# Expert stages of an eight-stage transformer stack: weights in 8 KB runs, the gather of the next pair inside this pair's products, the overflow blocks ahead of the last pair, the residual in the router

## The chip, the cores and the metric

The kernel runs on one core of one Trainium2 chip. Its time is the device time of one execution in microseconds (us). Before the change three runs gave a median of 2939.56 us (2938.95 to 2942.76).

## The reference

The model is a stack on 256 tokens of 1024 features: two layers of (feed-forward, token mix, feed-forward), then (state space mixer, mixture of experts) and (dilated attention, mixture of experts). The change lies in the two mixture stages alone. Each computes, with 32 experts of hidden size 512:

```python
g_w, g_idx = lax.top_k(jax.nn.softmax(g_logits, axis=-1), 1)        # one of 4 groups
e_logits = e_logits[jnp.arange(t), g_idx[:, 0]]                     # its 8 experts
e_w, e_idx = lax.top_k(jax.nn.softmax(e_logits, axis=-1), MOE_TOP_K)  # two of them
e_w = e_w / jnp.sum(e_w, -1, keepdims=True)
gates = (g_w * e_w).reshape(-1)
...
def expert_block(args):
    xb, e = args
    h = jax.nn.silu(xb @ w_gate[e]) * (xb @ w_up[e])
    return h @ w_down[e]
...
ffn = _hierarchical_moe(x, ...)
x = _layer_norm_2(DEEPNORM_ALPHA * x + ffn, ln_g[i, 1], ln_b[i, 1])
```

All weights are float32: three matrices of 2 MB for each expert, 201 MB for a stage.

## The kernel before, in words

Activations lie with features on partitions, `X["T"]` as 8 chunks of 128 features by 256 tokens, and as high and low parts `X["h"]`, `X["l"]`. A stage (`moe`) goes like this.

**Router.** Sixteen products per stage (L1302, L1303) make the logits while the chunks of x come out of the layer norm before; `lf` takes them to SBUF, `lgt` and `xtp` are transposes that put the logits and x itself with tokens on partitions (`xt`). From the choice of experts DVE works out `rk`, the place of each token in its expert's list, and `gt`, its weight. `warm` issues idle products on TensorE.

**Pairs.** The 32 experts go in 16 pairs (indices 0 to 15), each expert with 64 places. For a pair, `run` issues in program order:
- the gather `xgp` (L1455): x of the tokens in the two lists, by one-hot products with `ot`, in two halves of four 128x128 chunks. One logical product of 32-bit numbers is two records in the trace. Each half goes to `xg` by a copy on DVE (L1460). Before the first pair is done, it goes in pieces of one chunk, alternately on DVE and ScalarE;
- the transposes of the weighted lists, `ogp` (L1463), copied to `og` by ScalarE (L1465);
- the gate and up products (L1478) into the sums `gps` and `ups`: two halves of the features, in each half gates, then ups, four chunks each. The first expert uses columns 0 to 63 of the array and the second columns 64 to 127: `[128*64]` in the trace, the two alternating in the program and running at the same time in the trace;
- tanh on ScalarE (L188), two multiplications on DVE (L1493, L1494) into `t`, four transposes `htp` (L1497), a copy to `hT` on DVE (L1499);
- the down products `yp` (L1510), 16 logical products in two output halves, again two experts side by side, copied to `y` by ScalarE (L1519);
- `eacc` (L1535): eight products that add the weighted rows into the sums of the stage, which stay in PSUM.

PSUM holds four banks of sums, one each for `gps` and `ups`, and two buffers of one bank (pool `em`, tag `m`) that `xgp`, `ogp`, `htp` and `yp` share in turn. `xg` and `y` share one buffer (tag `xy`).

**Residual.** x times ALPHA is put into the sums by 16 products with `alphas` (L1437), issued inside pair 0, some around its `htp` and the rest behind its `yp`.

**Weights.** For a pair 12 tiles of 1 MB are loaded by SyncE (L1564 gate and up, L1571 down) into a ring of 21 buffers, whose order is `ORDER` (L23). The view `(c p) m -> p c m` puts rows p, p+128, ... on partition p, so one run in memory is one row: 2 KB of gate or up, 4 KB of down. A load waits until the products that read its buffer before are done.

**Overflow.** `more()` (an If with a loop over blocks, L1594) handles experts with more than 64 tokens. It is written after pair 10 (`MOREQ`). Its body takes six buffers of the ring when the program is built, executed or not; in this run no body is executed in either stage.

**Last pair.** In pair 15 the mean for the next layer norm (`meanp`) is worked out too, and the products into the sums are in high and low parts.

The order in which each engine gets its instructions is set when the program is built: a scheduler takes instructions by its own estimates of when each can start, so instructions that are written one after the other can be interleaved.

Of the kernel before, what the change touches and what calls it, by code (L numbers as in the profile page):

```python
# [10 lines left out]
F32 = mybir.dt.float32  # L11
# [20 lines left out]
W1 = 0  # L32
# [15 lines left out]
def tile_stack(ctx: ExitStack, tc: tile.TileContext, a: dict, out: bass.AP):  # L48
# [43 lines left out]
    def project_group(tiles, ws):  # L92
        """up to four chunks at once, (wh, wl, width) each; features outermost, so that it can start on the first."""
# [96 lines left out]
    def table(name):  # L190
        """the functions' tables, loaded behind the last tanh."""
# [4 lines left out]
    def warm(out, n, after):  # L196
        """the array's clock falls in a pause: idle products, into a sum not in use, keep it up."""
# [5 lines left out]
    def last_chunks(accs, ks, first):  # L203
        """the products of the last chunks, (wh, wl, mh, ml) each, into one output chunk."""
# [113 lines left out]
    def ffn(l, w1, w2, g, b, setup=None):  # L318
        with pool(name="accps", bufs=1, space=PSUM) as aps, pool(name="gups", bufs=2, space=PSUM) as gps, \
# [26 lines left out]
            def gate_up(js):  # L346
                """the hidden chunks js; features outermost, so that it can start on the first of them."""
# [42 lines left out]
    def log1p_exp_neg_abs(pool, x, shape, tag):  # L390
        """log(1 + exp(-|x|)) by the series of atanh."""
# [34 lines left out]
    def bias_tile(pool, h, queue=None, bufs=3):  # L426
        """T[q, k] = rel[bucket(128 + q - k), h], with the mask of the head's kind."""
# [48 lines left out]
    def token_mix(l):  # L476
        w_in, w_gate, w_out = a["w_in"][l], a["w_gate"][l], a["w_out"][l]
        with ExitStack() as st:
# [25 lines left out]
            def split_pair(t0, t1, c0):  # L504
                """stationary columns: 64 of t0, 64 of t1."""
# [19 lines left out]
            def k_pad(ps, kz, i):  # L525
                """a projected pair of keys into two tiles, each with zeros in the other's rows."""
# [10 lines left out]
            def v_tok(ps, v, i):  # L537
                """keys on partitions: v[:, tile, i, :]."""
# [7 lines left out]
            # compressed keys and values  # L546
# [28 lines left out]
            def compress(i, ts):  # L575
                """four products side by side, then their sum."""
# [26 lines left out]
            # compressed keys  # L603
# [23 lines left out]
            # compressed values  # L627
# [15 lines left out]
            # gates of the three branches and the forget gate  # L643
# [15 lines left out]
            # the running sums of the forget gates  # L659
# [9 lines left out]
            # attention over the compressed blocks, all heads at once  # L669
# [29 lines left out]
            def attend(q, kz, bias, sink=None, gate=None):  # L699
                """probabilities of one head, keys on partitions: [k0 x (q0 q1) | k1 x q1]."""  # L700
# [27 lines left out]
            def pv(po, jobs):  # L728
                """jobs[g]: list of (v of tile 0, v of tile 1 or None, probabilities)."""
# [55 lines left out]
            # NSA  # L785
# [17 lines left out]
            # sliding window with sinks  # L803
# [20 lines left out]
            # forgetting attention  # L824
# [79 lines left out]
    def rsqrt_tile(pool, v, eps, n=S):  # L904
        """(v + eps) ** -0.5, refined by a step of Newton's."""
# [9 lines left out]
    def ssd(g, b):  # L915
        w_in, w_out = a["ssd_w_in_2"][0], a["ssd_w_out_2"][0]
        with ExitStack() as st:
# [13 lines left out]
            def conv(ps, c, dst):  # L931
                """causal convolution of four taps, then twice its silu."""
# [9 lines left out]
            # the keys and queries of the states, B and C  # L942
# [6 lines left out]
            # steps, decays and their running sums  # L949
# [47 lines left out]
            def mix(j, xs, csb, y):  # L997
                """the states' sums for two heads."""
# [115 lines left out]
            # sin, with its sign by row, and cos, one where nothing turns  # L1114
# [136 lines left out]
    NE, CAP, HID, NOV = 32, 64, 512, 7  # L1251
    AHEAD = 7
    MOREQ = 10
# [18 lines left out]
    def router_parts(rp, l):  # L1272
        """the router's weights, high and low parts side by side."""
# [5 lines left out]
    def moe(l, g_, b_, rs, write=False):  # L1279
        w_g, w_u, w_d = a["moe_w_gate_2"][l], a["moe_w_up_2"][l], a["moe_w_down_2"][l]  # L1280
        with ExitStack() as st:
# [17 lines left out]
            # router  # L1299
            ps = mp.tile([72, S], F32, tag="m", name="lgp")  # L1300
            for c in range(KC):
# [7 lines left out]
            warm(accs[0][:, 0, :], W1, x)  # L1309
            # the groups' logits, filled up to eight, then the experts'  # L1310
# [7 lines left out]
            def top(x, name):  # L1318
                """the eight highest logits in order, and where they stand."""
# [8 lines left out]
            # the experts of the other groups far below  # L1328
# [8 lines left out]
            # which experts  # L1337
# [22 lines left out]
            warm(accs[0][:, 0, :], W2, x)  # L1360
# [6 lines left out]
            def weights():  # L1367
                """of the experts chosen."""
# [27 lines left out]
            def beyond():  # L1396
                """blocks of 64 places beyond an expert's first"""
# [33 lines left out]
            def residual():  # L1431
                """x * ALPHA, before the first pair."""
                if "r" not in done:
                    done["r"] = True
                    for c in range(KC):
                        for i in range(2):
                            x = nc.tensor.matmul(out=accs[c // 2][:, c % 2, i * 128:(i + 1) * 128], lhsT=xt[:, i, c * 128:(c + 1) * 128],  # L1437
                                                 rhs=alphas, start=(c % 2 == 0 and i == 0), stop=False, skip_group_check=True)
                            tc.add_manual_dep(x.ins, done["up"].ins.name, order, reason="gates first")

# [5 lines left out]
            def run(os, ogs, loads, n, last):  # L1446
                """n experts of 64 places: os[i], the places of the tokens of half i; ogs[i] with their weights."""
                P = n * CAP
                wg, wu, wd = loads
                xg = wk.tile([128, KC, 128], F32, tag="xy", name="xg", bufs=1)  # L1450
                for q in range(2):
                    ps = mp.tile([128, 4, 128], F32, tag="m", name="xgp")
                    for c in range(4):
# [3 lines left out]
                        if "r" not in done:  # L1457
                            first_copy(c % 2)(out=xg[:, q * 4 + c, 0:P], in_=ps[:, c, 0:P])
                    if "r" in done:
                        nc.vector.tensor_copy(out=xg[:, q * 4:q * 4 + 4, 0:P], in_=ps[:, :, 0:P])  # L1460
# [267 lines left out]
```

## Time and profile before

| | |
|---|---|
| median of 3 runs | 2939.56 us |
| span of the profiled execution | 2939.3 us |
| granted TensorE clock, mean | 0.988 |
| TensorE busy | 2802.7 us, 95% |
| VectorE, ScalarE, GpSimd busy | 1421.7, 1050.9, 196.5 us |
| bytes moved | 697 MB, 237 GB/s over the span |

The page gives for the profiled execution its span, from the first to the last instruction, and no time of its own beside it: 0.3 us under the median of the runs, so that terms of the trace can be added to either. The expert stages are the stretches from about 1684 to 2200 us and from about 2404 to 2920 us. In a row of the timeline the first two numbers are the start in us and the length of the (merged) records, and the bracket at its end is the idle time of the engine before it and what ended it. Matmuls are pipelined, and their ends are modelled, so the distance between starts is what a product costs.

### The profile page before, as it was taken

Reading aid. Unit: us, or ns where it says so; the run is one execution under the profiler, and the core shown is the slowest. Engines: PE = TensorE matmul, PEld = TensorE weight load, DVE = VectorE, ACT = ScalarE, POOL = GpSimd, SP = SyncE. Lnnn points to the kernel's source line nnn. Section 1 sums busy time; section 2 is a strip of 40 time slices with the busy share of each in tenths; the row PEclk is TensorE's granted clock in tenths of the full one; section 3 lists DMA queues with packets and bytes.
Section 4 is the critical chain, followed back from the end, with each engine's and each line's share of the span. In section 5 each row is a group of like instructions: output and inputs, shape, how many; then the busy total and the mean of one; then the engine's idle time right before and its main releaser. Section 6 shows DMA issues by size and latency. Waiting matters only on the chain. (4 is left out here: it accounts for less than half of the span.)

```text
span 2939.3 us, 46679 instructions
## 1 busy us (share of the span) xinstructions
PE 2802.7 (95%) x19161; PEld 2199.8 (75%) x19161; DVE 1421.7 (48%) x3075; ACT 1050.9 (36%) x1949; POOL 196.5 (7%) x263
## 2 busy tenths in 40 slices
PE   8899999999999999999999999999998989999998
PEld 8798899999999889999989854454448974444454
DVE  5466665755655765665688731111127762111113
ACT  4344555544544454544477510000015530000002
POOL 2102000200201100020100100000001010000000
PEclk9899999999999999999999999999999999999999
DMA  8666454455454745445455699998985479999896
GB/s 223 193 201 158 126 159 138 156 184 185 149 194 137 186 130 167 153 139 193 131 194 180 229 364 393 395 393 323 393 305 169 137 256 356 394 393 393 300 394 230
DMA packets 426793, 697.44 MB, mean 237 GB/s; under 512 B 19460, under 2 KB 238384, under 8 KB 426576
## 3 DMA queue, kind: packets, MB, share of 16 engines
q1 hardware_dynamic: 414976, 677.62, 66.3%
q10 hardware_dynamic: 9296, 11.66, 1.3%
q0 software_dynamic: 2304, 5.15, 1.2%
q8 instruction: 152, 2.49, 0.4%
q14 instruction: 65, 0.53, 0.1%
HBM read 693.25 MB, written 4.27 MB: 237 GB/s over the span
## 5 line engine op out<-in xcount | busy, mean ns | idle before, releaser
L84 DVE TENSOR_TENSOR whl<-w,whl 128x1024 fp32r<-128x1024 f32 x487 | 591.5, 1220 | 349.2 <-ACT whl L83 344.2
L83 ACT ACTIVATE whl<-w 128x1024 fp32r<-128x1024 f32 x487 | 507.3, 1050 | 355.9 <-PE gu L113 105.8
L111 PE MATMUL pp<-xh,whl 128*128 128x256 f32 x1432 | 418.1, 292 | 9.0 <-ACT xh L307 4.0
L112 PE MATMUL pp<-xl,whl 128*128 128x256 f32 x1432 | 418.7, 292 | 1.0 <-DVE xl L308 1.0
L113 PE MATMUL pp<-xh,whl 128*128 128x256 f32 x1432 | 412.8, 288 | 0.4 <-DVE whl L510 0.4
L111 PE MATMUL gu<-xh,whl 128*128 128x256 f32 x1408 | 401.6, 286 | 9.9 <-DVE h L361 7.2
L113 PE MATMUL gu<-xh,whl 128*128 128x256 f32 x1408 | 401.4, 285 | 0.5 <-DVE whl L84 0.5
L112 PE MATMUL gu<-xl,whl 128*128 128x256 f32 x1408 | 401.6, 285 | 0.0
L111 PEld LDWEIGHTS pp<-xh,whl 128*128 128x128 f32 x1432 | 274.6, 192 | 17.4 <-ACT xh L307 5.7
L112 PEld LDWEIGHTS pp<-xl,whl 128*128 128x128 f32 x1432 | 275.0, 192 | 10.0 <-issue 6.9
L111 PEld LDWEIGHTS gu<-xh,whl 128*128 128x128 f32 x1408 | 272.8, 194 | 12.2 <-ACT whl L83 9.4
L113 PEld LDWEIGHTS pp<-xh,whl 128*128 128x128 f32 x1432 | 274.6, 192 | 4.3 <-issue 2.4
L112 PEld LDWEIGHTS gu<-xl,whl 128*128 128x128 f32 x1408 | 273.0, 194 | 0.8 <-DVE xl L308 0.7
L113 PEld LDWEIGHTS gu<-xh,whl 128*128 128x128 f32 x1408 | 272.9, 194 | 0.8 <-DVE whl L84 0.8
L1460 DVE COPY xg<-xgp 128x512 f32<-128x512 f32 x60 | 41.5, 692 | 358.5 <-PE xgp L1455 358.5
L111 PE MATMUL acc<-hhi,whl 128*128 128x256 f32 x704 | 201.7, 287 | 2.4 <-DVE rT L231 2.2
L112 PE MATMUL acc<-hlo,whl 128*128 128x256 f32 x704 | 200.1, 284 | 0.0
L113 PE MATMUL acc<-hhi,whl 128*128 128x256 f32 x704 | 199.1, 284 | 0.0
L1493 DVE SCALAR_TENSOR_TENSOR t<-t,gps 128x512 f32<-128x512 f32 x32 | 22.0, 688 | 324.4 <-ACT t L188 324.4
L1519 ACT ACTIVATE y<-yp 128x512 f32<-128x512 f32 x60 | 35.8, 597 | 347.7 <-PE yp L1510 347.7
L111 PEld LDWEIGHTS acc<-hhi,whl 128*128 128x128 f32 x704 | 135.8, 193 | 5.4 <-DVE rT L231 4.0
L112 PEld LDWEIGHTS acc<-hlo,whl 128*128 128x128 f32 x704 | 135.8, 193 | 0.2
(571 smaller groups left out, 5063.0 us busy)
## 6 DMA issues: line engine op xcount, KB each, us to landing
w<-in_ffn_w_dram SPq DMA_DIRECT2D x130, 1024.0 KB, 5.3
wa<-in_moe_w_up_dram SPq DMA_DIRECT2D x48, 1024.0 KB, 14.2
whl<-in_moe_w_down_dram SPq DMA_DIRECT2D x47, 1024.0 KB, 14.1
wa<-in_moe_w_gate_dram SPq DMA_DIRECT2D x43, 1024.0 KB, 14.2
whl<-in_moe_w_gate_dram SPq DMA_DIRECT2D x39, 1024.0 KB, 14.1
wa<-in_moe_w_down_dram SPq DMA_DIRECT2D x37, 1024.0 KB, 13.4
whl<-in_moe_w_up_dram SPq DMA_DIRECT2D x36, 1024.0 KB, 14.2
w<-in_moe_w_down_dram SPq DMA_DIRECT2D x32, 1024.0 KB, 14.4
```

The costliest lines, as they stand in the source:

```text
L83: after_norm(nc.scalar.activation(out=hi, in_=w, func=AF.Copy), nc.vector.tensor_tensor(out=lo, in0=w, in1=hi.bitcast(F32), op=ALU.subtract))
L84: nc.vector.tensor_tensor(out=lo, in0=w, in1=hi.bitcast(F32), op=ALU.subtract))
L111: nc.tensor.matmul(out=o, lhsT=wh, rhs=xh, start=first, stop=False, skip_group_check=skip)
L112: nc.tensor.matmul(out=o, lhsT=wh, rhs=xl, start=False, stop=False, skip_group_check=skip)
L113: return nc.tensor.matmul(out=o, lhsT=wl, rhs=xh, start=False, stop=last, skip_group_check=skip)
L1460: nc.vector.tensor_copy(out=xg[:, q * 4:q * 4 + 4, 0:P], in_=ps[:, :, 0:P])
L1493: nc.vector.scalar_tensor_tensor(out=t[0:P], in0=t[0:P], scalar=1.0, in1=gps[0:P], op0=ALU.add, op1=ALU.mult)
L1519: nc.scalar.activation(out=y[0:P, hs], in_=yp[0:P], func=AF.Copy)
```

## The change

Four things are changed in the expert stages; elsewhere the diff only drops comments.

1. The view of the weights is `(p c) m -> p c m`: rows 4p to 4p+3 (gate, up; 2p and 2p+1 for down) lie on partition p, one run of 8 KB. Products then sum over features in another order, so the eviction of `xtp` to `xt` permutes (ScalarE reads PSUM with a stride of four), and `htp` transposes every second column of `t`.
2. The gather of pair q+1 is issued inside `run` of pair q: the first half behind the tanh, copied to `xg` by ScalarE, the second behind the copy to `hT`, copied by DVE. `ogp` comes behind `hT` (before the gates in the last pair alone). `y` moves to the buffers of `t` and `hT`, `xg` has one of its own.
3. `more()` stands ahead of pair 15, behind the last loads, and its gathered x takes a seventh buffer of the ring.
4. The residual is eight products of `alphas` with `X["T"]` (128x256) among the products of the router; the idle products ahead of them (`W1 = 0`) are gone, those behind (`W2`) write into a sum of their own.

```diff
             for c in range(KC):
                 nc.tensor.matmul(out=ps, lhsT=rs[:, c, :], rhs=X["h"][:, c, :], ...)
                 nc.tensor.matmul(out=ps[0:36], lhsT=rs[:, c, 0:36], rhs=X["l"][:, c, :], ...)
+                if c >= 2:
+                    residual(c - 2)
...
-                    nc.scalar.activation(out=xt[:, i, q * 512:(q + 1) * 512], in_=pt.rearrange("p c t -> p (c t)"), func=AF.Copy)
+                    nc.scalar.activation(out=xt[:, i, q * 512:(q + 1) * 512].rearrange("p (k f) -> p k f", k=4),
+                                         in_=pt.rearrange("p c t -> p (c t)").rearrange("p (f k) -> p k f", k=4), func=AF.Copy)
...
+            def gather(os, P, xg):
+                def half(q):
+                    ps = mp.tile([128, 4, 128], F32, tag="m", name="xgp")
+                    first = "r" not in done
+                    for c in range(4):
+                        for i in range(2):
+                            nc.tensor.matmul(out=ps[:, c, 0:P], lhsT=xt[:, i, (q * 4 + c) * 128:(q * 4 + c + 1) * 128], rhs=os[i], ...)
+                        if first:
+                            first_copy(c % 2)(out=xg[:, q * 4 + c, 0:P], in_=ps[:, c, 0:P])
+                    if not first:
+                        first_copy(1 - q)(out=xg[:, q * 4:q * 4 + 4, 0:P], in_=ps[:, :, 0:P])
+                return [lambda q=q: half(q) for q in range(2)]
...
                 tanh(out=t[0:P], in_=gps[0:P], scale=0.5)
+                if then:
+                    then.pop(0)()
...
-                    nc.tensor.transpose(ht[:, c, 0:P], t[0:P, c * 128:(c + 1) * 128], ident[0:P, 0:P])
+                    nc.tensor.transpose(ht[:, c, 0:P], t[0:P, c // 2 * 256 + c % 2:(c // 2 + 1) * 256:2], ident[0:P, 0:P])
                 hT = wk.tile([128, 4, 128], F32, tag="hT", name="hT", bufs=1)
                 nc.vector.tensor_copy(out=hT[:, :, 0:P], in_=ht[:, :, 0:P])
+                if then:
+                    then.pop(0)()
+                if not last:
+                    ogp = mp.tile([128, S], F32, tag="m", name="ogp")
...
-                residual()
+                done["r"] = True
                 for c in range(KC):
                     combine(c)
...
-    ... w[k][h * 512:(h + 1) * 512, :].rearrange("(c p) m -> p c m", p=128))
+    ... w[k][h * 512:(h + 1) * 512, :].rearrange("(p c) m -> p c m", p=128))
...
-                if q == MOREQ:
-                    more()
+                if q == NP - 1:
+                    more()
```

The order on TensorE shows what the scheduler makes of it. First a pair from the middle of a stage, from the end of one pair's sums (`eacc`) into the gates of the next; W names the buffer that a weight lies in (`w`, `wa`, `whl`), and a DMAHW wait is for its load. Before:

```order
L1535 MATMUL eacc_19046<-og,y 128x256 x2
L1455 MATMUL xgp<-ot,xtok 128x128 [waits PE_49]
L1455 MATMUL xgp<-ot,xtok 128x128 x7
L1455 MATMUL xgp<-ot,xtok 128x128 [waits PE_49]
L1455 MATMUL xgp<-ot,xtok 128x128 x7
L1463 MATMUL ogp<-ident,ogt 128x128 [waits DVE_49]
L1463 MATMUL ogp<-ident,ogt 128x128
L1478 MATMUL gps<-w,xg 64x512 [waits DMAHW1_49]
L1478 MATMUL gps<-w,xg 64x512 [waits DMAHW2_49]
L1478 MATMUL gps<-w,xg 64x512 x6
```

After, the gates of a pair with an index from 6 to 14 in the first expert stage (7 to 14 in the second):

```order
L1549 MATMUL eacc_19046<-og,y 128x256 x2
L1482 MATMUL gps<-whl,xg 64x512 [waits DMAHW5_49]
L1451 MATMUL xgp<-ot,xtok 128x128 [waits PE_49]
L1482 MATMUL gps<-whl,xg 64x512 [waits DMAHW6_49]
L1482 MATMUL gps<-whl,xg 64x512 x6
L1451 MATMUL xgp<-ot,xtok 128x128 x2
L1482 MATMUL ups<-whl,xg 64x512 [waits DMAHW7_49]
L1451 MATMUL xgp<-ot,xtok 128x128 x5
L1482 MATMUL ups<-whl,xg 64x512 [waits DMAHW0_49]
L1482 MATMUL ups<-whl,xg 64x512 x6
L1482 MATMUL gps<-whl,xg 64x512 [waits DMAHW1_49]
```

The first half of the next gather stands in pieces of one, two and five products inside the gate and up products, behind the first expert's first gate and first up product, ahead of the second expert's.

Second, the place behind the up products of a pair, before:

```order
L1497 MATMUL htp<-ident,t 128x128 [waits DVE_49,Activation_49]
L1497 MATMUL htp<-ident,t 128x128 x3
L1510 MATMUL yp<-xl,hT 64x512 [waits DMAHW5_49,DVE_49]
L1510 MATMUL yp<-wa,hT 64x512 [waits DMAHW6_49]
L1510 MATMUL yp<-xl,hT 64x512
```

After, in the same pairs as above:

```order
L1503 MATMUL htp<-ident,t 128x128 [waits DVE_49]
L1503 MATMUL htp<-ident,t 128x128 x3
L1451 MATMUL xgp<-ot,xtok 128x128 [waits Activation_49]
L1451 MATMUL xgp<-ot,xtok 128x128 x7
L1511 MATMUL ogp<-ident,ogt 128x128 [waits DVE_49]
L1511 MATMUL ogp<-ident,ogt 128x128
L1522 MATMUL yp<-wa,hT 64x512 [waits DMAHW5_49,Activation_49]
```

The second half of the gather and `ogp` now stand between `htp` and `yp`. In pairs 1 to 4 the first half stands whole between the up products and `htp`, and in pairs 1 to 3 (1 to 4 in the second stage) one gate product of the next pair's first expert alone stands between `ogp` and `yp`; in pair 0 three such products stand among the pieces of the gather. Where pairs 0 to 4 did so, the next pair's gates begin with the second expert.

Third, the end of the router's logits, before:

```order
L1302 MATMUL lgp<-xh,rs 72x256 [waits Activation_49]
L1303 MATMUL lgp<-xl,rs 36x256 [waits DVE_49]
L1308 MATMUL lgt<-ident,lf 128x72 [waits Activation_49]
L1308 MATMUL lgt<-ident,lf 128x72
L1349 MATMUL xtp<-ident,xT 128x128 [waits PE_49,Pool_49]
```

After:

```order
L1305 MATMUL lgp<-xh,rs 72x256 [waits Activation_49]
L1301 MATMUL eacc_19046<-xT,alphas 128x256 [waits Pool_49]
L1306 MATMUL lgp<-xl,rs 36x256 [waits DVE_49]
L1305 MATMUL lgp<-xh,rs 72x256 [waits Activation_49]
L1306 MATMUL lgp<-xl,rs 36x256 [waits DVE_49]
L1313 MATMUL lgt<-ident,lf 128x72 [waits Activation_49]
```

All eight residual products stand ahead of the last three products of the logits, and the last of them waits for the last chunk of `X["T"]`, which GpSimd writes.

## Rows read from the trace of the kernel before

**Rows 1.** Windows of a middle pair: PE, PEld, DVE, ACT, POOL busy, PEclk, DMA share, GB/s
```profile
1785.00:1815.00 30.00, 28.64 (x148) 13.84 (x149) 3.97 (x9) 2.17 (x4) 0.00 (x0) 1.00 1.04 394
```
**Rows 2.** Waits of PE, 1720 to 2190: in total, times, longest
```profile
PE htp L1497 <- DVE t L1494: 13.5, 15, 0.9
PE yp L1510 <- DVE hT L1499: 11.0, 14, 0.8
```
**Rows 3.** Timeline of ACT, tanh of pairs 0, 1, 3, 4, 14, 15 and 0, 15
```profile
1716.45 0.60 ACT L188 ACTIVATE t<-gps 128x512 f32<-128x512 f32 x1 [10.06 <-PE gps L1478]
1749.04 0.60 ACT L188 ACTIVATE t<-gps 128x512 f32<-128x512 f32 x1 [10.04 <-PE gps L1478]
...
1810.50 0.60 ACT L188 ACTIVATE t<-gps 128x512 f32<-128x512 f32 x1 [10.04 <-PE gps L1478]
1841.23 0.60 ACT L188 ACTIVATE t<-gps 128x512 f32<-128x512 f32 x1 [10.04 <-PE gps L1478]
...
2149.44 0.60 ACT L188 ACTIVATE t<-gps 128x512 f32<-128x512 f32 x1 [10.02 <-PE gps L1478]
2181.82 0.60 ACT L188 ACTIVATE t<-gps 128x512 f32<-128x512 f32 x1 [3.19 <-PE gps L1478]
...
2436.98 0.60 ACT L188 ACTIVATE t<-gps 128x512 f32<-128x512 f32 x1 [10.06 <-PE gps L1478]
...
2903.66 0.60 ACT L188 ACTIVATE t<-gps 128x512 f32<-128x512 f32 x1 [3.19 <-PE gps L1478]
```
**Rows 4.** Timeline of PE, one pair: gates to the next pair's gates
```profile
1799.90 3.65 PE L1478 MATMUL gps<-wa,xg 128*64 128x512 f32 x16
...
1813.27 0.59 PE L1478 MATMUL ups<-w,xg 128*64 128x512 f32 x1
1814.77 0.63 PE L1497 MATMUL htp<-ident,t 128*128 128x128 f32 x4 [0.91 <-DVE t L1494]
1816.18 4.08 PE L1510 MATMUL yp<-w,hT 128*64 128x512 f32 x17 [0.78 <-DVE hT L1499]
...
1823.20 3.72 PE L1535 MATMUL eacc<-og,y 128*128 128x256 f32 x16
1826.75 3.73 PE L1455 MATMUL xgp<-ot,xtok 128*128 128x128 f32 x32
1830.32 0.38 PE L1463 MATMUL ogp<-ident,ogt 128*128 128x128 f32 x2
1830.64 1.94 PE L1478 MATMUL gps<-wa,xg 128*64 128x512 f32 x8
```
**Rows 5.** Timeline of PE, pair 0: a gate product of one expert alone
```profile
1703.45 1.07 PE L1478 MATMUL gps<-wa,xg 128*64 128x512 f32 x2
1704.45 1.16 PE L1455 MATMUL xgp<-ot,xtok 128*128 128x128 f32 x8
...
1705.90 0.64 PE L1478 MATMUL gps<-w,xg 128*64 128x512 f32 x1
...
1719.78 1.16 PE L1437 MATMUL eacc<-alphas,xtok 128*128 128x128 f32 x8
```
**Rows 6.** Timelines of ACT and DVE, the copies behind `ogp` and `xgp`
```profile
1830.53 0.69 DVE L1460 COPY xg<-xgp 128x512 f32<-128x512 f32 x1
1830.80 0.38 ACT L1465 ACTIVATE og<-ogp 128x256 f32<-128x256 f32 x1 [6.87 <-PE ogp L1463]
```
**Rows 7.** Timelines of PE and POOL: the residual in pair 0, the router's end
```profile
1729.22 2.05 PE L1437 MATMUL eacc<-alphas,xtok 128*128 128x128 f32 x16
...
1683.57 9.03 POOL L310 TENSOR_SCALAR xT<-rT,pars 128x256 f32<-128x256 f32 x8 [2.02 <-DVE rT L302]
...
1691.59 0.43 PE L1303 MATMUL lgp<-xl,rs 128*36 128x256 f32 x1
...
1692.05 0.47 ACT L1305 ACTIVATE lf<-lgp,rb 72x256 f32<-72x256 f32 x1 [1.60 <-PE lgp L1303]
```
**Rows 8.** Window of the stall at `more()`, columns as in Rows 1
```profile
2010.00:2020.00 10.00, 10.00 (x65) 6.52 (x65) 1.38 (x2) 0.38 (x1) 0.00 (x0) 1.00 0.01 2
```

More of the change, by code (lines that the diff above doesn't have):

```diff
@@ L31 @@
 WARM = 10
-W1 = 0
 W2 = 4
@@ L1300, in moe, with residual @@
             ps = mp.tile([72, S], F32, tag="m", name="lgp")
+            def residual(c):
+                nc.tensor.matmul(out=accs[c // 2][:, c % 2, :], lhsT=alphas, rhs=X["T"][:, c, :], start=(c % 2 == 0), stop=False,
+                                 skip_group_check=True)
             for c in range(KC):
@@ L1308, in moe @@
                 x = nc.tensor.transpose(pt[:, i, :], lf[:, i * 128:(i + 1) * 128], ident[0:72, 0:72])
-            warm(accs[0][:, 0, :], W1, x)
+            for c in (KC - 2, KC - 1):
+                residual(c)
             lg = T([128, 2, 40], "lg")
@@ L1429, in beyond @@
                     nc.vector.tensor_tensor(out=rkb[:, i, 0:NOV], in0=rkb[:, i, 0:NOV], in1=base, op=ALU.subtract)
[L1431 to L1439, printed above, removed]
             done = {}
@@ L1456, in run @@
                                              start=(i == 0), stop=(i == 1))
-                        if "r" not in done:
+                        if first:
                             first_copy(c % 2)(out=xg[:, q * 4 + c, 0:P], in_=ps[:, c, 0:P])
-                    if "r" in done:
-                        nc.vector.tensor_copy(out=xg[:, q * 4:q * 4 + 4, 0:P], in_=ps[:, :, 0:P])
-                ogp = mp.tile([128, S], F32, tag="m", name="ogp")
-                for i in range(2):
-                    nc.tensor.transpose(ogp[0:P, i * 128:(i + 1) * 128], ogs[i], ident)
-                og = wk.tile([128, S], F32R if last else F32, tag="og", name="og", bufs=1)
-                nc.scalar.activation(out=og[0:P], in_=ogp[0:P], func=AF.Copy, scale=0.5)
-                if last:
+                    if not first:
+                        first_copy(1 - q)(out=xg[:, q * 4:q * 4 + 4, 0:P], in_=ps[:, :, 0:P])
+                return [lambda q=q: half(q) for q in range(2)]
+            def run(xg, ogs, loads, n, last, then=()):
+                P = n * CAP
+                wg, wu, wd = loads
+                then = list(then)
+                if last:
+                    ogp = mp.tile([128, S], F32, tag="m", name="ogp")
+                    for i in range(2):
+                        nc.tensor.transpose(ogp[0:P, i * 128:(i + 1) * 128], ogs[i], ident)
+                    og = wk.tile([128, S], F32R, tag="og", name="og", bufs=1)
+                    nc.scalar.activation(out=og, in_=ogp, func=AF.Copy, scale=0.5)
                     ogl = wk.tile([128, S], F32R, tag="ogl", name="ogl", bufs=1)
@@ L1516, in run @@
                     nc.vector.reduce_sum(out=ysum[:, 1:2], in_=yps[1], axis=AX.X)
+                if not last:
+                    ys = [wk.tile([128, 512], F32, tag=k, name="y", bufs=1) for k in ("t", "hT")]
                 for hf, yp in enumerate(yps):
                     hs = slice(hf * 512, (hf + 1) * 512)
-                    nc.scalar.activation(out=y[0:P, hs], in_=yp[0:P], func=AF.Copy)
+                    nc.scalar.activation(out=y[0:P, hs] if last else ys[hf][0:P], in_=yp[0:P], func=AF.Copy)
                     if last:
@@ L1587, in pair, with gather_pair @@
                     nc.vector.tensor_tensor(out=og, in0=o, in1=gt[:, i, 2 * q:2 * q + 2].unsqueeze(2).to_broadcast([128, 2, CAP]), op=ALU.mult)
[L1588 removed]
                     ogs.append(og.rearrange("p e s -> p (e s)"))
[L1590 removed]
+                return ogs
+            def gather_pair(os):
+                xg = wk.tile([128, KC, 128], F32, tag="xg", name="xg", bufs=1)
+                return xg, gather([o.rearrange("p e s -> p (e s)") for o in os], 2 * CAP, xg)
             def more():
@@ L1605, in more, with first_half @@
                             ogs.append(og)
-                        run(os, ogs, ld, 1, False)
-            for q in range(NE // 2):
-                last = pair(q)
+                        xg = next_tile([128, KC, 256])
+                        for f in gather(os, CAP, xg):
+                            f()
+                        run(xg, ogs, ld, 1, False)
+            NP = NE // 2
+            for q in range(NP):
+                ld = load([(w_g[e], w_u[e], w_d[e]) for e in (2 * q, 2 * q + 1)])
+                if q == 0:
+                    os = places(0)
+                    weights()
+                    xg, steps = gather_pair(os)
+                    for f in steps:
+                        f()
+                if q == NP - 1:
+                    more()
+                ogs = weighted(q, os)
+                steps = ()
+                if q < NP - 1:
+                    os = places(q + 1)
+                    hold = {}
+                    def first_half(os=os, hold=hold):
+                        hold["xg"], hold["steps"] = gather_pair(os)
+                        hold["steps"][0]()
+                    steps = (first_half, lambda hold=hold: hold["steps"][1]())
+                last = run(xg, ogs, ld, 2, q == NP - 1, steps)
+                if q < NP - 1:
+                    xg = hold["xg"]
                 if q == 1:
                     beyond()
-                if q == MOREQ:
-                    more()
             st4.close()
```

33 lines of the change are left out of this document (14 added, 19 removed).

## The prediction

> **What bounds the kernel now.** I read the windows first, then the waits of TensorE, then the tanh of each pair as a clock for the pairs, then one pair on TensorE row by row. In a middle pair TensorE is busy 28.64 of 30 us at the full clock (1.00), while the DMA engines are at share 1.04 and move 394 GB/s [rows 1]: both are close to their limits, and which one paces has to be found. The waits say TensorE: over a stage it waits 13.5 us for `t` (15 times up to 0.9) and 11.0 us for `hT` (14 times up to 0.8), both parts of its own chain, and no wait for a weight stands in that list [rows 2]. The pairs are regular to 0.01 us, 30.73 from tanh to tanh [rows 3], as a chain of instructions is and a stream of transfers is not. The transfers keep up only thanks to the ring: a pair takes 12 tiles of 1.049 MB, 12.58 MB, which in 30.74 us would be 409 GB/s against 394 moved; 15 pairs draw about 7 MB, 7 of the 21 buffers, from the lead.
>
> So a change is worth what it does to TensorE's chain within a pair. That chain, from the end of the gates E (last step's start 1813.27 plus the step of 0.43, 1813.70) [rows 4]: `htp` starts at +1.07, `yp` at +2.48, `eacc` at +9.50, the gather at +13.05, `ogp` at +16.62, the next gates at +16.94, and these take 13.80, sixteen steps of 0.86 in each of which both experts' products run side by side. Sum 30.74.
>
> **Weights in 8 KB runs.** Transfers aren't waited for, so a faster flow buys nothing; I count 0. What they could cost is bounded below. The stall at `more()`, whose six unused buffers leave the ring short until a window of 10 us moves 2 GB/s [rows 8], goes; its price is already small. With the first interval at 32.59 (1716.45 to 1749.04), the last at 32.38 (2149.44 to 2181.82) and 13 of 30.74 the first stage would take 464.6 from tanh 0 to tanh 15; it takes 465.4. The second takes 466.7 [rows 3]. So the stall costs 0.8 and 2.1 us. It goes wholly below, since I compare with these totals.
>
> **The gather inside the products.** Its intent is to cover the two waits, 1.7 us a pair. But the order shows gather products between a gate product of the first expert and that of the second. A product uses 64 columns; the gather uses all 128. So the split leaves the first expert's product alone, and the second's starts a step later with no partner at its end. The trace has one such place, in pair 0: the gate product that stands alone (two records) starts at 1703.45 and the gather goes on at 1704.45, 1.00 us, a full step of 0.86 and 0.14 for the changes; and what is left, from 1705.90 to 1719.78, still takes 13.88, not a step less than a whole pair [rows 5]. A lone product is a lost step.
>
> The Trainium skill (TensorEngine Tiling (Array Packing), Tiling Modes, Key Properties) says that a change of the tiling mode drains the engine, while tiles of one mode run independently. The 0.14 agree in sign. Without any such drain the sum below would be about 10 us smaller, 2966.
>
> I count four kinds of interval, E to E.
> - *Pairs 1 to 3 (second stage 1 to 4).* Half the gather (half of 3.57, 1.78) stands whole behind the gates and covers the wait for `t`: `htp` at +1.9, the second half at +2.8 (it waits for ScalarE's copy of the first), to +4.6, `ogp` 0.32, a lone gate product 1.0 to +5.95, `yp` 7.02, `eacc` 3.55, to +16.5; the gates still 13.80, because the second expert's sixteen products remain. 30.4, 0.3 less than before.
> - *Pairs 6 to 14 (7 to 14).* Behind the gates `htp` at +1.07 uncovered as before; the second half +1.53 to +3.3, `ogp` to +3.64; `yp` now needs the buffer that `ogp` leaves, a copy of 0.38 [rows 6] that starts some 0.2 later, so +4.24; `eacc` at +11.26, end +14.8. In the gates two lone products at 1.0, the other sixteen steps 13.80, and eight gather products in three pieces, 1.78 and about 0.1 for each further change, 2.1: 17.9. Together 32.8, 2.0 more.
> - *Pair 0 to 1.* The residual leaves: 16 records stood behind `yp` for 2.05 [rows 7], of which the last 0.2 overlaps what follows: 32.59 − 1.85 = 30.74. In come three lone products, 3.0, and about 1 for the gather in single chunks, each waiting for a copy; the `hT` wait (0.8) is covered: 33.9. Two lone products more ahead of pair 0's own gates stand where the gather waits for copies of single chunks: 0, at most 2.0 a stage.
> - *The rest.* Pair 4 to 5 has a long post without a lone product (16.1) and gates split once in the first stage (15.8): 31.9. Pair 5 to 6: 15.0 + 17.9 = 32.9; in the second stage 16.1 + 17.9 = 34.0. Pair 14 to 15 has no gather behind it: 14.8, about 0.5 for the branch, a lone product and `ogp` 1.35, 13.8, together 30.6.
>
> First stage: 33.9 + 3 × 30.4 + 31.9 + 32.9 + 8 × 32.8 + 30.6 = 482.9, against 465.4: +17.5. Second: 33.9 + 4 × 30.4 + 34.0 + 8 × 32.8 + 30.6 = 482.5, against 466.7: +15.8.
>
> **The residual in the router.** The last of its eight products stands ahead of three products of the logits and waits for the eighth chunk of `X["T"]`, which GpSimd ends at 1683.57 + 9.03 = 1692.6; the logits were done by 1692.05, where ScalarE takes them [rows 7]. Three products behind that, each 0.43 long where they last ran and overlapping a little, put `lf` at 1693.7, 1.65 later; the idle products that go ahead of the transposes of x give a little back: 1.4 later to the first gather. Two stages, +2.8. Bounds: −1 (the array is kept busier) to +2.5 each.
>
> **Costs that no row shows.** The weight loads of `htp` read every second column of `t`: 0 if the stride is free; if the four products, 0.63 as the row shows them with an overlapping end, took twice as long, about 0.5 a pair [rows 4], 15 us in all. All loads of before are contiguous; I take 0. The strided copies to `xt` are four a stage; the DVE copy of that size takes 0.69 [rows 6], so twice as long is +2.8 a stage. I take 0, the nearest rows being those of copies without a stride. The 8 KB runs must now bring 12.58 MB in 32.8 us, 384 GB/s, less than the 394 of today, so even a loss of 2% costs nothing.
>
> **The sum.** 17.5 + 15.8 + 2.8 = 36.1. Span 2939.3 + 36.1 = 2975.4; the median stands 0.3 above the span, so **2976 us**.
>
> **Rivals.**
> - *Lone products are hidden (faster).* If the array works off the lone product while the gather's weights are loaded, the 25 lone products of each stage cost nothing. At 1.0 each that is 50 us: 2926. The covered waits then count, and the flow must rise to some 414 GB/s or live on the ring. It decides where a lone product costs under about 0.3 us (36.1 / 50 taken from 1.0). For it: two experts' products do run at once. Against: 1703.45 to 1704.45. 7%.
> - *Half of it.* A lone product costs 0.3 to 0.4, so that losses and covered waits balance: about 2940. 6%.
> - *The transfers become the bound (slower still).* 201.3 MB a stage, 22 MB of them ahead in the ring: at 350 GB/s the rest takes 512 us against 482.9, so +29 a stage, 3034. It decides under about 370 GB/s. For it: DMA share 1.04, no room. Against: nothing in the rows says that longer runs flow slower. 5%.
> - *The stride of `htp` costs double.* 2976 + 15 = 2991. 7%.
>
> **How the numbers follow.** The forecast has 75%, with its own range of 2958 to 2990: the low end where changes of mode are free (−10) and the one-chunk gather and branch cost nothing (−5), the high end with the lone products at pair 0, the router and the copies at their upper bounds (+12) and a little stride. Taking in the stride rival gives 2957 to 2992, with 18% outside on both sides. A measurement of this kernel tells 0.2%, 6 us, from no change. Slower: 75 + 5 + 7 = 87%; same 6%; faster 7%.
>
> **What will show it.** Right: tanh to tanh 32.8 in the later pairs and 30.4 in pairs 1 to 4; lone records of `gps` and `ups` with a distance of about 1.0 to the gather behind them; no more `hT` wait on `yp`, a wait of some 0.6 on ScalarE's copy in its place; no window near zero GB/s inside a stage. Wrong: a middle interval under 31, waits of `gps` or `yp` for a DMA, or a longer `htp`.

## The result, and the profile after

The changed kernel took 2984.3 us (median of 4, 2983.67 to 2986.27) against 2940.72 us for the kernel before on the same chip: a ratio of 1.0153, 95% interval 1.0139 to 1.0168, or 43.6 us slower. The forecast was 2976 us, between 2957 and 2992. The span of the profiled execution grew from 2939.3 to 2982.3 us.

The tanh of the pairs shows where. Timeline of ScalarE after, the tanh (now L187) of pairs 0, 1, 2, 7, 8, 14, 15 of the first stage and 0, 15 of the second:

```profile
1715.10 0.60 ACT L187 ACTIVATE t<-gps 128x512 f32<-128x512 f32 x1 [9.31 <-PE gps L1482]
1748.63 0.60 ACT L187 ACTIVATE t<-gps 128x512 f32<-128x512 f32 x1 [12.70 <-PE gps L1482]
1778.95 0.60 ACT L187 ACTIVATE t<-gps 128x512 f32<-128x512 f32 x1 [13.46 <-PE gps L1482]
...
1938.65 0.60 ACT L187 ACTIVATE t<-gps 128x512 f32<-128x512 f32 x1 [18.03 <-PE gps L1482]
1971.84 0.60 ACT L187 ACTIVATE t<-gps 128x512 f32<-128x512 f32 x1 [18.03 <-PE gps L1482]
...
2170.98 0.60 ACT L187 ACTIVATE t<-gps 128x512 f32<-128x512 f32 x1 [18.03 <-PE gps L1482]
2201.36 0.60 ACT L187 ACTIVATE t<-gps 128x512 f32<-128x512 f32 x1 [7.71 <-PE gps L1482]
...
2461.51 0.60 ACT L187 ACTIVATE t<-gps 128x512 f32<-128x512 f32 x1 [9.31 <-PE gps L1482]
...
2946.85 0.60 ACT L187 ACTIVATE t<-gps 128x512 f32<-128x512 f32 x1 [7.71 <-PE gps L1482]
```

The early pairs take 30.3 us (1748.63 to 1778.95), the later ones 33.19 (1938.65 to 1971.84), the first interval 33.53, the last 30.38. Where a stage goes over from the one kind to the other, one interval takes 35.75 us in the first stage (pair 5 to 6) and 35.63 in the second (6 to 7): three lone products fall into it, since the up products behind the tanh of the pair ahead are split as well (at 1869.40 and 2649.21). From tanh 0 to tanh 15 a stage takes 486.3 and 485.3 us, against 465.4 and 466.7 in [rows 3]: +20.9 and +18.7. The rest is small: the kernel arrives at the first router 3.4 us earlier, the first router takes 2.1 and the second 3.6 us longer, the attention stage between them 1.3 longer. Together 43.2, less 0.2 at the end: 43.0 in the span. The median stands 2.0 above this span.

The 3.4 us are not the change's, and the 1.3 can't be told from none: the stretch between the stages, from the last tanh to GpSimd's chunks, is 222.3 us before and 223.6 after, and 219.6 to 224.1 in the other profiled executions. The instructions of TensorE ahead of the first router are the same in both kernels, and the chunks of `X["T"]` on GpSimd, which start at 1683.57 in [rows 7], start between 1678.5 and 1681.9 in the twelve other profiled executions of this study.

The waits of TensorE after, 1720 to 2200 us, answer to [rows 2]:

```profile
PE htp L1503 <- DVE t L1500: 7.0, 9, 0.8
PE yp L1522 <- ACT og L1513: 5.2, 11, 0.5
PE xgp L1451 <- ACT xg L1442: 1.1, 5, 0.2
```

The wait for `hT` is gone, that for `t` is covered in the early pairs and stays in the nine later ones, and a wait of 0.5 for the copy of `og` has come. 24.5 us of waits have become 13.3: the change does what it says, and TensorE is busier (96%) with the same work. The cost is therefore in the products. TensorE after, one later pair, from `htp` into the next gates, answers to [rows 4]:

```profile
1942.77 0.74 PE L1503 MATMUL htp<-ident,t 128*128 128x128 f32 x4 [0.78 <-DVE t L1500]
1943.35 1.95 PE L1451 MATMUL xgp<-ot,xtok 128*128 128x128 f32 x16
1945.14 0.38 PE L1511 MATMUL ogp<-ident,ogt 128*128 128x128 f32 x2
1945.99 7.14 PE L1522 MATMUL yp<-whl,hT 128*64 128x512 f32 x32 [0.47 <-ACT og L1513]
1953.06 3.72 PE L1549 MATMUL eacc<-og,y 128*128 128x256 f32 x16
1956.71 1.07 PE L1482 MATMUL gps<-whl,xg 128*64 128x512 f32 x2
1957.71 0.49 PE L1451 MATMUL xgp<-ot,xtok 128*128 128x128 f32 x2
1958.13 3.65 PE L1482 MATMUL gps<-whl,xg 128*64 128x512 f32 x14
1961.71 0.71 PE L1451 MATMUL xgp<-ot,xtok 128*128 128x128 f32 x4
1962.35 1.07 PE L1482 MATMUL ups<-whl,xg 128*64 128x512 f32 x2
1963.35 1.38 PE L1451 MATMUL xgp<-ot,xtok 128*128 128x128 f32 x10
```

Look at the two rows of `gps` and `ups` with x2: each is one product of one expert (two records) and takes 1.00 us to the gather behind it (1956.71 to 1957.71, 1962.35 to 1963.35), as in [rows 5]. The gather's half, 1.78 when whole before, takes 0.42 + 0.64 + 1.31 = 2.37 in three pieces.

Windows after (columns as in [rows 1]): one later pair, and the place where [rows 8] has 2 GB/s:

```profile
1905.50:1938.70 33.20, 31.95 (x152) 14.75 (x150) 3.56 (x8) 2.78 (x6) 0.00 (x0) 1.00 0.96 379
2010.00:2020.00 10.00, 9.53 (x53) 4.67 (x52) 2.12 (x6) 1.39 (x3) 0.00 (x0) 1.00 0.98 382
```

379 GB/s, less than the 394 of before, is no sign of a slower flow: 12.58 MB in 33.19 us are 379 GB/s, so the loads now wait for TensorE, and among the waits of TensorE in this stage no load stands. The hole of `more()` is closed.

### The profile page after: what moved, and what is told of

It reads as the page before. It is cut to its first block, busy times and chain, and to the rows that moved or that the text cites. A ratio compares the mean times of both kernels' runs of the same rounds, so it can differ in the third digit from the quotient of the medians.

```text
span 2982.3 us, 46603 instructions
## 1 busy us (share of the span) xinstructions
PE 2871.5 (96%) x19129; PEld 2215.6 (74%) x19129; DVE 1402.3 (47%) x3051; ACT 1071.0 (36%) x1985; POOL 196.5 (7%) x263
## 5 line engine op out<-in xcount | busy, mean ns | idle before, releaser
L187 ACT ACTIVATE t<-gps 128x512 f32<-128x512 f32 x32 | 19.1, 597 | 489.3 <-PE gps L1482 489.3
L1451 PEld LDWEIGHTS xgp<-ot,xtok 128*128 128x128 f32 x1024 | 123.6, 192 | 70.3 <-issue 47.1
L1451 PE MATMUL xgp<-ot,xtok 128*128 128x128 f32 x1024 | 142.5, 284 | 2.1 <-ACT xg L1442 2.1
```

What stands on the lines that cost most here:

```text
L187: last_tanh.append(nc.scalar.activation(out=out, in_=in_, func=AF.Tanh, **kw))
L1451: nc.tensor.matmul(out=ps[:, c, 0:P], lhsT=xt[:, i, (q * 4 + c) * 128:(q * 4 + c + 1) * 128], rhs=os[i], start=(i == 0), stop=(i == 1))
```

## The experiments

**What each part does alone.** First the residual alone, on the kernel before:

```diff
+                if c >= 2:
+                    residual(c - 2)      # alphas x X["T"], among the router's products
-                residual()               # behind yp of pair 0
```

> The kernel before with the residual alone moved to the router. Theory A (the loss of 43.6 us comes from the order of the gate products that the moved gather brings): about no change, the first interval from tanh to tanh 1.8 us shorter in each stage and the router about 2 us longer, 2938 to 2942 us. Theory B (the router is the loss: residual products wait for GpSimd ahead of the logits): 5 us or more a stage, 2950 us or more.

Measured 2939.68 us, ratio 0.9997 (0.9988 to 1.0006): no change. The first interval falls from 32.59 to 30.71 us, and from the start of GpSimd's chunks to tanh 0 it takes 1.5 us more in the first stage and 2.7 in the second. Theory B falls.

Then the long runs, with the residual in the router:

```diff
-    ... .rearrange("(c p) m -> p c m", p=128)
+    ... .rearrange("(p c) m -> p c m", p=128)    # with the strided copies of x and columns of t
```

> The kernel before with the residual in the router and the weights in 8 KB runs (strided copy of x, strided transposes of t), the gather and the overflow blocks where they were. Theory A: as the run with the residual alone to within 4 us, 2934 to 2942 us, since TensorE paces; middle intervals 30.7 to 30.8 us; a higher flow where a load is not held back. Theory C (the long runs or the strided reads are the loss): htp longer, intervals 31.5 us or more, 2965 us or more.

Measured 2948.54 us, ratio 1.0033 (1.0021 to 1.0045), 8.9 us above the run with the residual alone: more than theory A allowed, far less than theory C. The intervals are 30.82 us instead of 30.73, and `htp` 0.71 or 0.72 instead of 0.63: the strided weight loads cost 0.09 a pair here, some 3 us in all. Single intervals are 1.7 us longer still, such as 32.52 from pair 1 to 2. There the granted clock fell. Windows of this run (columns as in [rows 1]) and its TensorE rows at that place, two of each kind:

```profile
1745.00:1750.00 5.00, 3.45 (x18) 1.26 (x14) 1.98 (x3) 0.00 (x0) 0.00 (x0) 1.00 1.00 419
1750.00:1752.00 2.00, 1.86 (x6) 0.65 (x8) 1.93 (x8) 0.00 (x0) 0.00 (x0) 0.66 1.01 426
1752.00:1754.00 2.00, 2.00 (x6) 0.48 (x4) 1.93 (x8) 0.00 (x0) 0.00 (x0) 0.50 0.99 418
```

```profile
1748.64 0.72 PE L1497 MATMUL htp<-ident,t 128*128 128x128 f32 x4 [0.91 <-DVE t L1494]
1750.14 0.65 PE L1510 MATMUL yp<-xl,hT 128*64 128x512 f32 x1 [0.78 <-DVE hT L1499]
...
1751.45 1.06 PE L1510 MATMUL yp<-xl,hT 128*64 128x512 f32 x1
...
1752.30 1.06 PE L1510 MATMUL yp<-xl,hT 128*64 128x512 f32 x1
```

Half a step takes 0.85 instead of 0.43 (1751.45 to 1752.30), behind the two waits of 0.91 and 0.78; it comes four times in the two stages of this execution, once in the run with the residual alone, once in the run that splits the gates (below), and in no pair of the kernel before or of the changed one. So the long runs add 8.9 us where both waits are uncovered; what they cost where the waits are covered is measured below. That a gap only 0.09 longer tips the clock is not shown, since most pairs with the same gap kept it.

The overflow blocks alone, on the kernel before:

```diff
-                if q == MOREQ:
-                    more()
+                if between is not None:      # more, handed to pair 15 behind its loads
+                    between()
```

> The kernel before with the overflow blocks alone moved, from behind pair 10 to ahead of pair 15, behind the last loads. Theory A: the stall of the loads goes and with it 0.6 us in the first and 2.1 us in the second stage; the branch costs about 0.5 us at its new place: 2937 to 2941 us, no change that can be told. Rival I (the branch or the six buffers now hold back pair 15 or the next stage's loads): 2 us or more a stage, 2944 us or more.

Measured 2932.79 us, ratio 0.9975 (0.9964 to 0.9985): faster, and by more than expected. The stall is gone (intervals of 30.78 at its place in both stages), and the last interval fell too, 31.30 instead of 32.37, which I had not foreseen and whose cause stays open; 1.6 and 2.9 us in the stages. The interval of the ratio begins at 4.4 us, which these make; the median's further 3.6 us are not accounted for, and are smaller than the 5 us by which executions differ ahead of the first router.

The gather alone, the other three parts undone:

```diff
+                if then:
+                    then.pop(0)()        # a half of the next gather, behind the tanh; again behind hT
```

> The changed kernel with three of the four changes undone (2 KB and 4 KB runs, overflow blocks behind pair 10, residual in pair 0): the gather alone is moved. Theory A: nearly the whole loss stays, intervals of 33.2 us in the later pairs, 2972 to 2988 us. Theories B and C: the gather is a gain by itself, 1.0 to 1.7 us a pair, 2890 to 2910 us.

Measured 2972.83 us, ratio 1.0104 (1.0089 to 1.0120), +32 us; the later intervals are 33.10 us. Theory A holds: this part, meant to cover waits, is the loss. The changed kernel's 11 us on top are its 0.09 a pair, the longer routers, and single intervals; they were not taken apart further.

**Lone products by themselves.** On the kernel before, the two `ogp` transposes go between the first gate products of the two experts:

```diff
+    if e == 0: lists()                                    # ogp, behind the first expert's first product
+    else: tc.add_manual_dep(done["up"].ins, done["og"].ins.name, order, reason="split")
```

> The kernel before with one thing more: in every pair but the last of a stage the two transposes of ogp stand between the first gate product of the first expert and that of the second, instead of ahead of both. No work is added. Theory A: a lone product costs a step, 0.86 us and 0.1 to 0.2 for the changes, so intervals of 31.7 us instead of 30.73 and about 30 us in all, 2970 us. Rival D (a lone product is hidden behind the transposes and the second expert's products): intervals of 30.7 to 30.8 us, 2940 us.

Measured 2968.77 us, ratio 1.0094 (1.0079 to 1.0110): +28 us with no work added. Timeline of TensorE of this run, a middle pair:

```profile
1797.92 1.07 PE L1486 MATMUL gps<-wa,xg 128*64 128x512 f32 x2
1798.92 0.44 PE L1466 MATMUL ogp<-ident,ogt 128*128 128x128 f32 x2
1799.29 3.22 PE L1486 MATMUL gps<-wa,xg 128*64 128x512 f32 x13
```

The lone product takes 1.00 us, and the intervals are 31.82 us, 1.09 above [rows 3]. Rival D falls: in these rows nothing runs beside the product on 64 columns when the next one wants all 128.

**The gather kept whole.** One line on the changed kernel:

```diff
+    tc.add_manual_dep(x.ins, done["up"].ins.name, order, reason="gates first")   # x: each gather product
```

> The changed kernel with one thing more: the gather products may not stand ahead of the pair's last up product, so both halves stay whole. Theory A (split gates are the loss): the later pairs fall from 33.2 us to about 29.9 (no lone products, the wait for t covered), 453 and 455 us from tanh 0 to tanh 15 of a stage instead of 486 and 485, 2920 us. Rival E (the loss is the wait for the copy of og or the gather's contention, and stays): 33 us a pair, 2980 us. Rival F (the transfers set a floor of 12.58 MB a pair at about 394 GB/s, 31.9 us): 2945 us or more.

Measured 2924.64 us, ratio 0.9944 (0.9928 to 0.9961): 59.7 us below the changed kernel, 15.5 below the one before. TensorE in a middle pair of this run:

```profile
1930.46 3.60 PE L1484 MATMUL ups<-wa,xg 128*64 128x512 f32 x16
1934.00 2.05 PE L1451 MATMUL xgp<-ot,xtok 128*128 128x128 f32 x16
1935.88 0.64 PE L1505 MATMUL htp<-ident,t 128*128 128x128 f32 x4
1936.73 2.05 PE L1451 MATMUL xgp<-ot,xtok 128*128 128x128 f32 x16 [0.21 <-ACT xg L1442]
1938.62 0.38 PE L1513 MATMUL ogp<-ident,ogt 128*128 128x128 f32 x2
1939.48 7.14 PE L1524 MATMUL yp<-whl,hT 128*64 128x512 f32 x32 [0.47 <-ACT og L1515]
```

`htp` follows the first half without a wait, and the pair takes 30.08 us. The 3.11 us to 33.19 add up: two lone products 2.00, the half in pieces 0.49 (2.37 for 1.88), the wait for `t` 0.78, less 0.21 for the wait of the second half, 3.06. Rivals E and F fall; the flow rose to 412 to 420 GB/s in windows of 50 us up to 2100 us, and no load stands among the waits.

The gate products side by side in every pair but the last:

```diff
+    if h + c == 0 and k in done:      # k: "sum" (last eacc) or "xg" (last gather product)
+        tc.add_manual_dep(done["up"].ins, done[k].ins.name, order, reason="side by side")
```

> The same, and the first gate product of a pair may not stand ahead of the sums of the pair before (for pair 0, of its gather): no lone product is left. Theory A: 29.9 us in every pair and three lone steps fewer between pairs 0 and 1, 2909 us, 10 us less than with the gather whole alone. Rival D (lone products in a wait cost nothing): as the gather whole alone, 2920 us.

Measured 2914.96 us, ratio 0.9911 (0.9894 to 0.9927): 10 us less, as theory A has it. Two lone products are in fact left in each stage: one of `yp` among the pieces of the gather in pair 0 (1.00 us), and one gate product of pair 15 (0.97). The early pairs gain only 0.3 (30.34 to 30.03); most comes ahead of pair 0 and between pairs 0 and 1 (33.53 to 31.95). For the early pairs rival D was right but for the 0.3, and the changed kernel shows why, at one of them:

```profile
1786.86 0.38 PE L1511 MATMUL ogp<-ident,ogt 128*128 128x128 f32 x2
1787.17 1.07 PE L1482 MATMUL gps<-wa,xg 128*64 128x512 f32 x2
1787.72 7.39 PE L1522 MATMUL yp<-whl,hT 128*64 128x512 f32 x32
```

The lone gate product is followed by `yp`, which uses 64 columns as well. It starts 0.55 later, not 1.00; but it starts 0.86 behind `ogp`, and in the later pairs, with no lone product between, 0.85 (1945.14 to 1945.99), because it waits 0.47 for `og`. So the lone product lies in a wait, and whether `yp` could have run beside it without that wait no run separates.

The same with the short runs and without strides:

```diff
-    ... .rearrange("(p c) m -> p c m", p=128)
+    ... .rearrange("(c p) m -> p c m", p=128)
```

> The kernel without lone products, with the weights in 2 KB and 4 KB runs and no stride in the copies of x and the transposes of t. A pair then needs 421 GB/s. Theory G (long runs matter once TensorE asks for more than the 394 GB/s that the short runs bring): waits of gps or yp for loads, or idle slots, late in each stage, 5 to 15 us more than with long runs. Theory H (the ring's lead of 21 buffers lasts for the stage): 0.09 us a pair less, 2 to 4 us faster than with long runs.

Measured 2915.99 us, ratio 0.9919 (0.9902 to 0.9936), as with long runs: theory H in part. No load is waited for beyond 0.3 us, but the 0.09 that the missing stride should give isn't there (30.08 in both). TensorE in a middle pair of this run:

```profile
1930.35 0.60 PE L1508 MATMUL htp<-ident,t 128*128 128x128 f32 x4
1931.20 2.05 PE L1450 MATMUL xgp<-ot,xtok 128*128 128x128 f32 x16 [0.25 <-ACT xg L1441]
```

Directly behind the gather `htp` takes 0.60 without the stride and 0.64 with it, and the wait for ScalarE's copy that follows is longer by as much, 0.25 for 0.21: the second half starts 0.85 behind `htp` in both. Where the waits are covered, the long runs and the stride make no difference that can be told.

**Beyond both kernels.** On the kernel with the gates side by side, `ogp` goes back ahead of the gates:

```diff
-                if not last:
-                    ogp = ...          # behind hT
+                ogp = ...              # ahead of the gates, in every pair
```

> The kernel without lone products, with ogp ahead of the gates in every pair, as in the kernel before, so that yp no longer waits for the copy of og (0.5 us a pair). Theory A (TensorE's chain is all that counts): 29.3 us a pair, 2893 us. Rival F (the transfers take over: 12.58 MB in 29.3 us is 429 GB/s, over the 400 to 425 GB/s seen with long runs): waits for loads, 2900 us or more.

Measured 2896.87 us, ratio 0.9851 (0.9835 to 0.9868). The wait of `yp` is gone, a pair takes 29.54 us, 0.2 above the estimate, and no load is waited for: theory A. With short runs:

> The kernel with whole halves, no lone products and ogp ahead of the gates (29.5 us a pair), with the weights in 2 KB and 4 KB runs. A pair now asks for 426 GB/s, the short runs bring about 394. Theory G (long runs matter once TensorE asks for more): 192 tiles less 21 in the ring at 394 GB/s are 455 us, against 447 from tanh 0 to tanh 15 and some 14 us ahead of it: loads are waited for late in the stage, 2 to 10 us more than the 2897 us with long runs. Theory H (the lead lasts): 2894 to 2897 us.

Measured 2898.28 us, ratio 0.9855 (0.9840 to 0.9870): as with long runs, theory H, and the waits for loads of theory G are not there. Windows of 100 us, first of the run with short runs, then of that with long ones:

```profile
1800.00:1900.00 100.00, 99.25 (x507) 46.69 (x504) 12.40 (x26) 8.91 (x16) 0.00 (x0) 1.00 1.04 394
```

```profile
1800.00:1900.00 100.00, 99.15 (x520) 49.11 (x518) 14.19 (x30) 9.51 (x17) 0.00 (x0) 1.00 1.01 421
```

Long runs do flow faster, 421 against 394 GB/s. At 29.54 us a pair asks for 426, so the short runs live on the ring, and its 21 buffers last for the stage. Last, pair 1's gather in two copies instead of eight:

```diff
+                    done["r"] = True      # behind pair 0's own gather
```

> The same with long runs, and the gather of pair 1 copied in two halves instead of eight chunks inside pair 0. Theory A: the interval from pair 0 to pair 1 falls from 31.95 to 29.5 us in each stage, 5 us in all, 2892 us. Rival (the ring is not yet filled behind pair 0, so loads are waited for): 2897 us.

Measured 2894.23 us, ratio 0.9847 (0.9833 to 0.9860), the lowest median, though the interval overlaps that of the long runs above (0.9851). The trace shows the gain of theory A: the first interval is 29.61 us in both stages instead of 31.95, and the lone `yp` product in pair 0 is gone with the pieces of the gather.

## Why the prediction was right

**What bounds.** Right. Outside the stall at `more()`, TensorE's chain paced the pairs before, after and in every experiment, down to 29.5 us a pair; the transfers never took over.

**Lone products.** The mechanism and its place were right: two lone steps of 1.00 in the later pairs, forecast at 1.0. The run that only splits the gates confirms the price. It was wrong to charge 1.0 also in the early pairs, where the lone product lies in the wait of `yp` for `og` and `yp` starts 0.55 behind it; `yp` then took 7.32 (1787.72 to 1795.04) for 7.02 and the sums a little more, so that 30.34 came out where 30.4 was forecast, partly by luck. Without the lone product these pairs take 30.03: it costs 0.3 there.

**The later pairs.** Mis-sized: 32.8 forecast, 33.19 measured, 0.39 in each of 15, 6 us and the largest part of what the forecast lacked. The intervals where the stages go over came out as their sum: 30.07 and 35.75 for 31.9 and 32.9 in the first stage, 32.12 and 35.63 for 34.0 and 32.8 in the second, 1.0 more in each. The terms: `htp` to the second half 0.58 for 0.46, the strided weight loads among it (0 forecast, about 0.1 measured); `eacc` 3.65 for 3.55, into the lone product; the pieces 2.37 for 2.1. I had counted 0.1 for a change between 64 and 128 columns only inside the gates.

**The changes of mode.** The Trainium skill (TensorEngine Tiling (Array Packing), Tiling Modes, Key Properties) has each change of the tiling mode drain the engine. The pieces of the gather, 0.49 longer for four more changes, agree: about 0.1 each. No run here separates the drain from the other costs of a switch.

**The first interval.** 33.9 forecast, 33.53 measured, by luck. Three lone gate products were charged 3.0, and the run with the gates side by side gives back 1.58. A fourth, of `yp`, was not counted:

```profile
1726.57 1.07 PE L1522 MATMUL yp<-whl,hT 128*64 128x512 f32 x2
1727.57 0.71 PE L1451 MATMUL xgp<-ot,xtok 128*128 128x128 f32 x4
```

The gather in single chunks, charged about 1, costs 2.34 together with that product (31.95 against 29.61).

**The residual and the router.** To the first product of the gather the residual costs what was forecast: 1.5 us in the first stage for 1.4. Of the rows below the first is the kernel before, where GpSimd's chunks start at 1683.57 [rows 7], the other two the kernel after:

```profile
1699.85 1.05 PE L1455 MATMUL xgp<-ot,xtok 128*128 128x128 f32 x8
```

```profile
1680.13 9.04 POOL L309 TENSOR_SCALAR xT<-rT,pars 128x256 f32<-128x256 f32 x8 [2.02 <-DVE rT L301]
1697.91 1.74 PE L1451 MATMUL xgp<-ot,xtok 128*128 128x128 f32 x12
```

From the chunks to the gather it takes 16.28 us before and 17.78 after. No idle products gave anything back: `W1` is 0 in the kernel before as well. The two lone products more ahead of pair 0, counted at 0 and bounded by 2.0, make the difference of 0.6 from there to tanh 0 (16.60 and 17.19; 0.4 in the second stage). The run with the gather alone agrees: from the chunks to tanh 0 it takes 0.6 and 0.5 us more than the kernel before. In the second stage 1.7 us come on top, and the router leaves the bound of 2.5: the granted clock fell behind the wait for `mk`, and the idle products took 3.66 us, against 1.97 before. TensorE after, and the window:

```profile
2439.76 0.38 PE L1363 MATMUL rkp<-mk,tri 128*128 128x32 f32 x2 [0.93 <-DVE mk L1348]
...
2440.86 3.66 PE L198 MATMUL idle<-ones,ones 128*128 128x256 f32 x8
```

```profile
2440.00:2445.00 5.00, 5.00 (x24) 4.28 (x24) 2.57 (x16) 0.00 (x0) 0.00 (x0) 0.66 0.91 372
```

In the first stage the clock gained instead, but TensorE then waits 0.85 for `mk`, so the gather starts no earlier for it. Windows before and after:

```profile
1690.00:1695.00 5.00, 3.73 (x16) 2.59 (x17) 3.38 (x18) 2.00 (x6) 2.60 (x3) 0.51 0.73 240
```

```profile
1690.00:1695.00 5.00, 2.78 (x22) 1.86 (x19) 3.71 (x30) 3.39 (x8) 0.00 (x0) 1.00 1.01 415
```

**The costs that no row showed.** The stride of `htp` costs 0.09 a pair where `htp` stands behind a wait, not 0 and far from the 0.5 of its bound. The 8 KB runs gained nothing, as forecast, even where they flow faster. The stall at `more()` was priced about right (0.8 and 2.1 us; the run with the overflow blocks alone gives back 0.5 and 1.9), but the last interval had 1.1 more in it. The 0.5 for the branch ahead of pair 15 has no row in any run: there the last interval only fell.

**The rivals.** Hidden lone products: false where a product on all columns follows; where `yp` follows, all but 0.3 is hidden, in a wait. Half the price: false. The transfers as the bound: false, no load was waited for in the later pairs of the changed kernel, and the long runs brought 421 GB/s where TensorE asked for 426. A double price for the stride: false.

**The sum.** The forecast is 8 us low. The span grew by 43.0 us for 36.1: the two stages by 39.6 for 33.3, the two routers by 5.7 for 2.8, less 2.3 elsewhere. The rest is the step from span to median, 2.0 us for the 0.3 that was taken from the kernel before. Some intervals of the forecast are also 0.1 higher than the terms written beside them (14.8 and 17.9 make 32.7, 16.5 and 13.8 make 30.3, the last comes to 30.45), 2 to 3 us in all, which hid as much of the mis-sizing.

**What was missed.** The stretch ahead of the first router differs by some 5 us between executions, nearly the 6 us that were to count as a change.

## What to carry to other kernels

When work is moved into a stretch so that it covers a wait, look at the order in which the scheduler puts it there: a product on all columns between two that run side by side on half of them costs a whole step, here 1.0 us for each place where TensorE doesn't wait anyhow. Tie moved work to the end of the group with an ordering edge; here one line turned a loss of 1.5% into a gain of 0.6%, and with the two places that it uncovered next 1.5%. A faster transfer was worth nothing here, because the ring of buffers carried the slower one through the stage.

## What the runs showed of the hardware beyond that

- A lone product on 64 columns takes 1.00 us to a following product on 128 columns. The one place where products on 64 columns follow lies in a wait (0.55 us to the next, which would have started there without it), so it gives no price.
- Loads of weights with a stride of two elements lengthen four transposes from 0.63 to 0.71 us behind a wait, and from 0.60 to 0.64 us behind other products.
- Over 100 us, 1 MB loads in runs of 8 KB moved 421 GB/s beside a TensorE that asked for 426; in runs of 2 and 4 KB 394.
- Behind two gaps of 0.91 and 0.78 us the granted clock fell once in a while to 0.50, the lower of its two levels (1.2 of 2.4 GHz), and cost 1.7 us; most pairs with the same gaps kept 1.00.
